# Stick-breaking weights with the query in the partitions: key sums by a scan on VectorE, and the logarithms transposed

## The chip, the core and the metric

The kernel runs on one core of one Trainium2 chip. The metric is the device time of one execution in microseconds; the median of three runs of the kernel before is 400.91 (400.55 to 401.03).

## What is computed

Two layers over 256 tokens of width 1024. In each layer a mixer of three groups of heads (block-sparse attention "moba", differential attention "diff", stick-breaking attention), gated and projected back, then a cross-attention to 256 memory tokens; at the end an RMS norm. The part that changes is stick-breaking, with 6 heads of width 64:

```
def stick_breaking_attention(q, k, v):
    """A[t,s] = sigmoid(z_ts) * prod_{s<j<t} (1 - sigmoid(z_tj)), strictly causal, no positions."""
    ...
        z = jnp.einsum('bhqd,bhkd->bhqk', qi, k).astype(jnp.float32) * scale
        mask = kpos[None, :] < (q0 + jnp.arange(Q_BLOCK))[:, None]
        log_beta = jax.nn.log_sigmoid(z)
        log_1m_beta = jnp.where(mask, log_beta - z, 0.0)
        between = lax.cumsum(log_1m_beta, axis=3, reverse=True) - log_1m_beta
        w = jnp.where(mask, jnp.exp(log_beta + between), 0.0)
        return jnp.einsum('bhqk,bhkd->bhqd', w.astype(v.dtype), v)
```

So each score z needs the sum of softplus(z) over the keys from its own to the query: the logarithm of the weight is z less that sum.

## The kernel before

Nearly all of TensorE's work is the big projections. Each weight granule (128 x 1024, float32, 512 KB) is loaded by SP into `wraw`, rounded by ScalarE into `whi` (L156), and VectorE computes the residual `wlo = wraw - whi` (L157); a product then takes three instructions (whi with the rounded activation, wlo with it, whi with the activation's residual). `wraw` has 5 buffers, `whi` and `wlo` 6 each, and granules are asked for five ahead. In `t_stationary` (L455 to L457, the token-major projections T0 to T3) a granule is 12 products of 512 columns.

TensorE's order is written out by hand: the projections call `tick` after each few products with the nanoseconds they took, and `tick` runs the steps of the attention jobs that are due. A job is a Python generator; each `yield` gives TensorE's time of the step and the wait until the next one is due (`SB_WAIT`, `PT_WAIT` and so on, in nanoseconds, L58 to L72). The other engines' orders come from the framework's scheduler, and each engine works through its own in order.

A stick-breaking job `sb(c, last)` (L745) does one pair of heads: three per layer, so six in all. Its steps are:

- `stick_banks` (L619): four score products in float32 into two banks of PSUM, with the key in the partitions and the query along the row (128 x 384: 256 queries for the first 128 keys, the later 128 for the rest), and a mask added by a product with an identity (L633).
- `softplus` (L637): per bank four Exp, Ln and Abs instructions on ScalarE (L642 to L646), three on VectorE (L647 to L649), and a split into a rounded part `sbh` (ScalarE) and a residual `sbl` (VectorE, L170).
- `stick_weights` (L655): the sum over keys goes down the partitions, so it is a product with a triangle of -1 (`trim`, L659) and, across the two key blocks, with a full matrix of -1 (`allm`, L660), for both parts, added on top of the scores in the same bank; then an Exp to SBUF gives the weights (`pt`).
- `pv` (L602): the product with the values, for all waiting pairs together.

The diff and moba attentions (`score_quad`, `score_banks`, `numerators`) have the query in the partitions; their probabilities are transposed by TensorE in `p_transposed` (L591): three 128 x 128 transposes into a bank and a copy. The tiles `sbe`, `sby` and so on come from the pool `work`, which has two buffers of each name.

Of the kernel before, what the change touches and what calls it, by code (L numbers as in the profile page):

```python
# [15 lines left out]
OP = mybir.AluOpType  # L16
# [4 lines left out]
KT = 8  # L21
NEG = -1.0e30
# [36 lines left out]
SB_WAIT, SB_PACE = 8000, 9000  # L59
# [18 lines left out]
class Trunk:  # L78
# [94 lines left out]
    def constants(self):  # L173
# [3 lines left out]
        self.identR = C.tile([128, 128], R, name="identR")  # L177
        nc.gpsimd.tensor_copy(self.identR, self.ident)
        tmp = self.work.tile([128, 256], F32, name="ctmp", tag="sq")

        self.cmask = C.tile([128, 384], F32, name="cmask")
        nc.gpsimd.memset(self.cmask, 0.0)
        for c in (0, 256):
            nc.gpsimd.affine_select(self.cmask[:, c:c + 128], self.cmask[:, c:c + 128], [[-1, 128]],
                                    OP.is_ge, NEG, base=0, channel_multiplier=1)

        nc.gpsimd.memset(tmp, 0.0)
        for c in (0, 128):
            nc.gpsimd.affine_select(tmp[:, c:c + 128], tmp[:, c:c + 128], [[1, 128]],
                                    OP.is_gt, NEG, base=0, channel_multiplier=-1)  # L190
        self.smask = C.tile([128, 256], R, name="smask")
        nc.gpsimd.tensor_copy(self.smask, tmp)

        tri = C.tile([128, 128], F32, name="trif")
        nc.gpsimd.memset(tri, -1.0)
        self.allm = C.tile([128, 128], R, name="allm")
        nc.gpsimd.tensor_copy(self.allm, tri)

        self.halfm = C.tile([128, 128], R, name="halfm")
        half = self.work.tile([128, 256], F32, name="ctmp2", tag="sq")  # L200
        nc.gpsimd.memset(half[:, 0:128], -1.0)
# [3 lines left out]
        nc.gpsimd.affine_select(tri, tri, [[-1, 128]], OP.is_ge, 0.0, base=0, channel_multiplier=1)  # L205
        self.trim = C.tile([128, 128], R, name="trim")
        nc.gpsimd.tensor_copy(self.trim, tri)
# [348 lines left out]
    def score_banks(self, qa, ka, qb, kb):  # L556

        a, b = self.bank(), self.bank()
        near = lambda ps, q, k: self.nc.tensor.matmul(ps[:, 0:128], q[:, 0:128], k[:, 0:128], start=True, stop=True)
        far = lambda ps, q, k: self.nc.tensor.matmul(ps[:, 128:384], q[:, 128:256], k, start=True, stop=True)  # L560
        near(a, qa, ka)
        far(b, qb, kb)
        far(a, qa, ka)
        near(b, qb, kb)
        return a, b

    def score_quad(self, qk):

        banks = [self.bank() for _ in qk]
        for a, b in ((0, 128), (128, 256)):  # L570
            for ps, (q, k) in zip(banks, qk):
                self.nc.tensor.matmul(ps[:, a:a + b], q[:, a:a + 128], k[:, 0:b], start=True, stop=True)
        return banks

    def numerators(self, ps, scale):
# [4 lines left out]
        for t, c in ((0, slice(0, 128)), (1, slice(128, 384))):  # L580
# [4 lines left out]
        for t, c in ((0, slice(0, 128)), (1, slice(128, 384))):  # L585
# [5 lines left out]
    def p_transposed(self, p):  # L591
# [6 lines left out]
        with self.urgent():  # L598
            nc.scalar.activation(pt[:, 0:384], ps[:, 0:384], AF.Copy)
        return pt  # L600

    def pv(self, v, pts):  # L602
# [16 lines left out]
    def stick_banks(self, qa, ka, qb, kb):  # L619

        nc = self.nc
        a, b = self.bank(), self.bank()
        kw = dict(skip_group_check=True)
        near = lambda ps, q, k, s: nc.tensor.matmul(ps[:, 0:256], k[:, 0:128], q, start=s, stop=False, **kw)
        far = lambda ps, q, k, s: nc.tensor.matmul(ps[:, 256:384], k[:, 128:256], q[:, 128:256], start=s, stop=False,
                                                   **kw)
        far(a, qa, ka, True)
        near(b, qb, kb, True)
        near(a, qa, ka, False)
        far(b, qb, kb, False)  # L630
        for ps in (a, b):
            diagonal = ps.rearrange("p (b c) -> p b c", c=256)[:, :, 0:128]
            nc.tensor.matmul(diagonal, self.identR, self.smask, start=False, stop=True, **kw)  # L633
        return a, b

    def softplus(self, ps):

        nc = self.nc
# [7 lines left out]
        nc.scalar.activation(r, y, AF.Exp, scale=-1.0)  # L646
        nc.vector.scalar_tensor_tensor(r, e, 1.0, r, OP.add, OP.mult)  # L647
        nc.vector.scalar_tensor_tensor(r, r, -1.0, y, OP.add, OP.add)
        nc.vector.scalar_tensor_tensor(e, z, 0.0, r, OP.max, OP.add)  # L649
        self.split(e, hi, lo)  # L650
        return ps, hi, lo

    def stick_weights(self, ps, hi, lo):

        nc = self.nc  # L655
        kw = dict(skip_group_check=True)
        z = ps[:, 0:384]
        for p in (hi, lo):
# [478 lines left out]
```

## Time and profile before

| what | value |
|---|---|
| median of the runs | 400.91 us |
| profiled execution, its own time | 399.81 us |
| its span, first to last instruction | 398.1 us |
| TensorE busy | 390.6 us, 2803 products |
| VectorE busy | 320.8 us, 784 instructions |
| ScalarE busy | 282.4 us, 593 instructions |
| granted TensorE clock, mean | 0.999 |

The profile is of one execution. Busy time counts an engine's instructions, with overlaps once; a product's recorded length includes its drain, so what a product costs the stream is the distance from its start to the next one's. "Idle before" a row names what ended the wait of that engine. A chain of waits leads back from the last instruction to what released it.

### The profile page before, as it was taken

What the parts mean: (1) busy time and instruction counts of PE and PEld (TensorE: products, weight loads), DVE (VectorE), ACT (ScalarE), POOL (GpSimd) and SP (SyncE); (2) the same over time, 40 slices, a digit from 0 to 9 for tenths busy, and PEclk for the clock granted to TensorE, in tenths of its full rate; (3) what the DMA queues carried; (4) which work ended last, traced back from release to release, by engine and by line L of the source; (5) the groups of instructions that cost most, each with busy time, mean ns of one, the idle gap of its engine ahead of it and who ended that gap; (6) DMA issues with size and microseconds to landing.
All of it is one profiled execution on the core that took longest, in us unless ns stands there. A gap on an engine that the chain in (4) does not pass through costs nothing.

```text
span 398.1 us, 7706 instructions
## 1 busy us (share of the span) xinstructions
PE 390.6 (98%) x2803; PEld 355.2 (89%) x2803; DVE 320.8 (81%) x784; ACT 282.4 (71%) x593; POOL 43.7 (11%) x109
## 2 busy tenths in 40 slices
PE   8999999999999999999999999999999999999993
PEld 8999988777899989988999999888788999998983
DVE  5988868788969869889797864876997896797964
ACT  7889588776866868559486934879687667675843
POOL 5688950000000000000000000000000000000000
PEclk9999999999999999999999999999999999999999
DMA  8995794334353343721747765443346433361002
GB/s 287 351 321 173 244 314 151 132 108 138 131 186 130 107 156 109 239 80 53 265 121 267 242 210 169 160 158 105 94 154 225 132 120 127 108 212 53 1 2 105
DMA packets 19190, 64.10 MB, mean 161 GB/s; under 512 B 2384, under 2 KB 2768, under 8 KB 19152
## 3 DMA queue, kind: packets, MB, share of 16 engines
q1 hardware_dynamic: 19152, 63.61, 47.2%
q8 instruction: 22, 0.36, 0.4%
q14 instruction: 16, 0.13, 0.1%
HBM read 62.55 MB, written 1.05 MB: 160 GB/s over the span
## 4 chain that ended last, share of the span: by engine, by line
PE 89%; DVE 6%; ACT 3%; issue 1%; ACTq 0%; DVEq 0%
PE bank L428 39%; PE bank L455 8%; PE bank L457 7%; PE bank L456 7%; PE bank L1013 3%; PE bank L607 2%; PE bank L596 2%; DVE wlo L157 2%; PE bank L948 1%; PE bank L659 1%; ACT whi L156 1%; PE bank L765 1%; PE bank L483 1%; PE bank L482 1%; PE bank L481 1%
## 5 line engine op out<-in xcount | busy, mean ns | idle before, releaser
L157 DVE TENSOR_TENSOR wlo<-wraw,whi 128x1024 fp32r<-128x1024 f32 (+2 forms) x118 | 137.3, 1169 | 33.8 <-ACT whi L156 32.3
L156 ACT ACTIVATE whi<-wraw 128x1024 fp32r<-128x1024 f32 (+2 forms) x118 | 118.2, 1011 | 40.0 <-PE bank L428 19.5
L428 PE MATMUL bank<-xh,whi 128*128 128x256 f32 x416 | 119.1, 287 | 0.0
L428 PE MATMUL bank<-xh,wlo 128*128 128x256 f32 x416 | 117.3, 283 | 0.0
L428 PE MATMUL bank<-xl,whi 128*128 128x256 f32 x416 | 117.1, 283 | 0.0
L428 PEld LDWEIGHTS bank<-xh,whi 128*128 128x128 f32 x416 | 79.4, 191 | 1.4 <-issue 0.7
L428 PEld LDWEIGHTS bank<-xh,wlo 128*128 128x128 f32 x416 | 79.5, 192 | 0.2 <-DVE wlo L157 0.2
L428 PEld LDWEIGHTS bank<-xl,whi 128*128 128x128 f32 x416 | 79.5, 192 | 0.0
L455 PE MATMUL bank<-whi,xh 128*128 128x512 f32 x128 | 52.0, 407 | 0.0
L456 PE MATMUL bank<-wlo,xh 128*128 128x512 f32 x128 | 50.1, 392 | 0.0
L457 PE MATMUL bank<-whi,xl 128*128 128x512 f32 x128 | 50.1, 391 | 0.0
L586 ACT ACTIVATE prob<-prob,mx 128x128 f32<-128x128 f32 (+1 forms) x56 | 24.8, 445 | 10.9 <-DVE mx L583 10.9
L455 PEld LDWEIGHTS bank<-whi,xh 128*128 128x128 f32 x128 | 24.1, 188 | 6.2 <-issue 2.0
L457 PEld LDWEIGHTS bank<-whi,xl 128*128 128x128 f32 x128 | 24.0, 188 | 5.3
L456 PEld LDWEIGHTS bank<-wlo,xh 128*128 128x128 f32 x128 | 24.1, 188 | 4.1
L314 ACT ACTIVATE xh<-h 128x256 fp32r<-128x256 f32 x32 | 14.5, 497 | 6.6 <-DVE h L310 6.3
L428 PE MATMUL bank<-mh,whi 128*128 128x256 f32 x64 | 18.8, 294 | 0.0
L581 DVE CUSTOM_DVE_ANT_0 prob<-bank,cmask 128x128 f32<-128x128 f32 (+1 forms) x56 | 17.9, 350 | 0.3
L428 PE MATMUL bank<-ml,whi 128*128 128x256 f32 x64 | 18.1, 282 | 0.0
L428 PE MATMUL bank<-mh,wlo 128*128 128x256 f32 x64 | 18.1, 282 | 0.0
L325 ACT ACTIVATE sq<-h 128x256 f32<-128x256 f32 x28 | 11.4, 410 | 6.4 <-DVE sqacc L326 5.9
L647 DVE SCALAR_TENSOR_TENSOR sbr<-sbe,sbr 128x384 f32<-128x384 f32 x12 | 6.4, 556 | 11.7 <-ACT sbr L646 11.7
(285 smaller groups left out, 790.2 us busy)
## 6 DMA issues: line engine op xcount, KB each, us to landing
wraw<-in_w_dram SPq DMA_DIRECT2D x107, 512.0 KB, 3.8
wraw<-in_w_dram SPq DMA_DIRECT2D x10, 256.0 KB, 4.4
wraw<-in_memT_dram SPq DMA_DIRECT2D x4, 512.0 KB, 4.6
h<-in_xT_dram SPq DMA_DIRECT2D x3, 256.0 KB, 4.5
out_dram<-wraw SPq DMA_DIRECT2D x2, 288.0 KB, 2.2
wraw<-in_gfin_dram SPq DMA_DIRECT2D x1, 512.0 KB, 4.9
out_dram<-wraw SPq DMA_DIRECT2D x2, 224.0 KB, 2.2
h<-in_xT_dram SPq DMA_DIRECT2D x1, 280.0 KB, 3.0
```

The costliest lines, as they stand in the source:

```text
L156: nc.scalar.activation(hi[:, c], raw[:, c], AF.Copy)
L157: nc.vector.tensor_tensor(lo[:, c], raw[:, c], hi[:, c].bitcast(F32), OP.subtract)
L314: nc.scalar.activation(h, src[k], AF.Copy, scale=g)
L325: nc.scalar.activation(s, src[k], AF.Square)
L428: nc.tensor.matmul(outs[m], st[:, kk, c], x[k], start=k + p == 0 and m % 2 == 0, stop=k == n - 1 and p == 2, skip_group_check=True)
L455: nc.tensor.matmul(outs[t], xh[k][:, c], whi[:, kk, :], start=first, stop=False)
L456: nc.tensor.matmul(outs[t], xh[k][:, c], wlo[:, kk, :], start=False, stop=False)
L457: nc.tensor.matmul(outs[t], xl[k][:, c], whi[:, kk, :], start=False, stop=last)
L581: nc.vector.tensor_tensor_reduce(s[:, c], ps[:, c], self.cmask[:, c], 1.0, -3.0e38, OP.add, OP.max, accum_out=m[:, t:t + 1])
L586: nc.scalar.activation(s[:, c], s[:, c], AF.Exp, bias=m[:, t:t + 1], scale=scale, accum_out=sm[:, t:t + 1])
L596: nc.tensor.transpose(ps[:, b * 128:b * 128 + 128], p[:, b * 128:b * 128 + 128], self.ident)
L1013: nc.tensor.matmul(out[:, 0:w], x[:, r], w_, start=m == 0 and not seeded, stop=m == 11, skip_group_check=True)
```

## The change

Stick-breaking's scores are made with the query in the partitions and the key along the row, by the same `score_banks` that moba uses. The tokens are laid out backwards on the host (input, positions, and output turned around), so that the sum from a key to the query becomes a running sum along the row; all other masks and block positions are turned to match, in `SEG`. `stick_logs` takes the place of `softplus`: VectorE adds the mask to the scores as it reads the bank (`sbz`), ScalarE does Abs, Exp, Ln, Exp and a Relu, VectorE two combining instructions, then one scan per query block (`tensor_tensor_scan` over Relu and the rest, 256 and 128 columns), and the subtract from the scores. The logarithms are then transposed by TensorE, and the instruction that takes them out of PSUM is an Exp (`p_transposed` with `AF.Exp`). Products with the mask, with `trim` and `allm`, and the split in two parts are gone. `SB_WAIT` goes from 8000 to 9000, the wait before the value products from `PT_WAIT` (950) to `SB_PT` (1300), and the job's stated TensorE times from 1070 and 1070 to 760 and 660.

```
+SEG = (0, slice(0, 256)), (1, slice(256, 384))
...
-SB_WAIT, SB_PACE = 8000, 9000
+SB_WAIT, SB_PACE, SB_PT = 9000, 9000, 1300
...
     def score_banks(self, qa, ka, qb, kb):
         a, b = self.bank(), self.bank()
-        near = lambda ps, q, k: self.nc.tensor.matmul(ps[:, 0:128], q[:, 0:128], k[:, 0:128], start=True, stop=True)
-        far = lambda ps, q, k: self.nc.tensor.matmul(ps[:, 128:384], q[:, 128:256], k, start=True, stop=True)
+        near = lambda ps, q, k: self.nc.tensor.matmul(ps[:, 256:384], q[:, 128:256], k[:, 128:256], start=True, stop=True)
+        far = lambda ps, q, k: self.nc.tensor.matmul(ps[:, 0:256], q[:, 0:128], k, start=True, stop=True)
...
-    def p_transposed(self, p):
+    def p_transposed(self, p, func=AF.Copy):
...
-            nc.scalar.activation(pt[:, 0:384], ps[:, 0:384], AF.Copy)
+            nc.scalar.activation(pt[:, 0:384], ps[:, 0:384], func)
...
-    def softplus(self, ps):
+    def stick_logs(self, ps):
         nc = self.nc
-        z = ps[:, 0:384]
-        W = lambda n, dt=F32: self.work.tile([128, 384], dt, name=n)
-        e, y, r, hi, lo = W("sbe"), W("sby"), W("sbr"), W("sbh", R), W("sbl", R)
+        W = lambda n: self.work.tile([128, 384], F32, name=n)
+        z, e, y, r, u = W("sbz"), W("sbe"), W("sby"), W("sbr"), W("sbu")
+        nc.vector.tensor_tensor(z, ps[:, 0:384], self.smask, OP.add)
         nc.scalar.activation(e, z, AF.Abs)
         nc.scalar.activation(e, e, AF.Exp, scale=-1.0)
         nc.scalar.activation(y, e, AF.Ln, bias=1.0)
         nc.scalar.activation(r, y, AF.Exp, scale=-1.0)
+        nc.scalar.activation(u, z, AF.Relu)
         nc.vector.scalar_tensor_tensor(r, e, 1.0, r, OP.add, OP.mult)
         nc.vector.scalar_tensor_tensor(r, r, -1.0, y, OP.add, OP.add)
-        nc.vector.scalar_tensor_tensor(e, z, 0.0, r, OP.max, OP.add)
-        self.split(e, hi, lo)
-        return ps, hi, lo
-
-    def stick_weights(self, ps, hi, lo):
...
+        for _, c in SEG:
+            nc.vector.tensor_tensor_scan(y[:, c], u[:, c], r[:, c], 0.0, OP.add, OP.add)
+        nc.vector.tensor_tensor(z, z, y, OP.subtract)
+        return z
...
         def sb(c, last):
             qk = [x[64 * j:64 * j + 64] for j in range(2) for x in (sqk[c], sqk[3 + c])]
-            z = [self.softplus(ps) for ps in self.stick_banks(*qk)]
-            yield 1070, SB_WAIT
-            w = [self.stick_weights(*x) for x in z]
-            yield 1070, PT_WAIT
+            z = [self.stick_logs(ps) for ps in self.score_banks(*qk)]
+            yield 760, SB_WAIT
+            w = [self.p_transposed(x, AF.Exp) for x in z]
+            yield 660, SB_PT
...
-    x = tr(f("x")[0]).reshape(128, 4, 512)
+    x = tr(f("x")[0][::-1]).reshape(128, 4, 512)
```

VectorE's order in the changed kernel, layer 0, from the second pair's first combining step to its last subtract (`sbz_1093` and `sbz_1109` are the pair's two banks; the two rows to `sby` of 256 and 128 columns are the scans of a bank; `wlo` rows belong to the projections):

```order
L619 SCALAR_TENSOR_TENSOR sbr_1096<-sbe_1094,sbr_1096 128x384
L620 SCALAR_TENSOR_TENSOR sbr_1096<-sbr_1096,sby_1095 128x384
L622 SCALAR_TENSOR_TENSOR sby_1095<-sbu_1097,sbr_1096 128x256
L622 SCALAR_TENSOR_TENSOR sby_1095<-sbu_1097,sbr_1096 128x128
L619 SCALAR_TENSOR_TENSOR sbr_1112<-sbe_1110,sbr_1112 128x384
L623 TENSOR_TENSOR sbz_1093<-sbz_1093,sby_1095 128x384
L620 SCALAR_TENSOR_TENSOR sbr_1112<-sbr_1112,sby_1111 128x384
L159 TENSOR_TENSOR wlo_1179<-wraw_1177,whi_1178 128x1024
L622 SCALAR_TENSOR_TENSOR sby_1111<-sbu_1113,sbr_1112 128x256
L622 SCALAR_TENSOR_TENSOR sby_1111<-sbu_1113,sbr_1112 128x128
L159 TENSOR_TENSOR wlo_1197<-wraw_1195,whi_1196 128x1024
L623 TENSOR_TENSOR sbz_1109<-sbz_1109,sby_1111 128x384
```

The same place before, from the second pair's first combining step to the residuals of its two banks:

```order
L647 SCALAR_TENSOR_TENSOR sbr_1116<-sbe_1114,sbr_1116 128x384
L647 SCALAR_TENSOR_TENSOR sbr_1130<-sbe_1128,sbr_1130 128x384
L648 SCALAR_TENSOR_TENSOR sbr_1116<-sbr_1116,sby_1115 128x384
L648 SCALAR_TENSOR_TENSOR sbr_1130<-sbr_1130,sby_1129 128x384
L649 SCALAR_TENSOR_TENSOR sbe_1114<-bank_1106,sbr_1116 128x384
L649 SCALAR_TENSOR_TENSOR sbe_1128<-bank_1107,sbr_1130 128x384
L157 TENSOR_TENSOR wlo_1184<-wraw_1182,whi_1183 128x1024
L170 TENSOR_TENSOR sbl_1118<-sbe_1114,sbh_1117 128x384
L170 TENSOR_TENSOR sbl_1132<-sbe_1128,sbh_1131 128x384
```

Between the combining steps and a bank's end there was one `wlo`; now there are two, and the second bank's end stands behind both.

VectorE's order in the changed kernel just ahead of that, from the first pair's last rows to the second pair's mask adds (L612, which read the score banks):

```order
L159 TENSOR_TENSOR wlo_1038<-wraw_1036,whi_1037 128x1024
L623 TENSOR_TENSOR sbz_1002<-sbz_1002,sby_1004 128x384
L159 TENSOR_TENSOR wlo_1071<-wraw_1069,whi_1070 128x1024
L536 TENSOR_TENSOR rp1_1128<-tq_1125,cosr_250 128x128
L388 COPY rbcm_1157<-bank_1154 128x256
L612 TENSOR_TENSOR sbz_1093<-bank_1087,smask_125 128x384
L612 TENSOR_TENSOR sbz_1109<-bank_1088,smask_125 128x384
```

The mask adds are new on this engine; they stand behind the first pair's last subtract, a weight residual, a product of the rotary embedding and a copy.

TensorE's order in the changed kernel, from the third pair's scores in layer 0 to the transposes of the second pair (`ident,sbz`), and what follows:

```order
L547 MATMUL bank<-sqk_687,sqk_684 128x128
L548 MATMUL bank<-sqk_687,sqk_684 128x256 x2
L547 MATMUL bank<-sqk_687,sqk_684 128x128
L443 MATMUL bank<-whi,xh_292 128x512
L444 MATMUL bank<-wlo,xh_292 128x512
L445 MATMUL bank<-whi,xl_293 128x512
L443 MATMUL bank<-whi,xh_292 128x512
L444 MATMUL bank<-wlo,xh_292 128x512
L445 MATMUL bank<-whi,xl_293 128x512
L584 MATMUL bank<-ident,sbz 128x128 x6
L725 MATMUL bank<-ident,tq 128x128 x4
```

Before, the mask product (L633) followed the scores, and in the place of the six transposes stood eight products with `trim` and `allm`. The scores of the next pair stand six big products ahead of a pair's transposes. In layer 0 the first pair's transposes stand at the like place behind the second pair's scores, where before the eight products came ahead of those scores.

## Rows read from the trace of the kernel before

**Rows 1.** The page, part 1: busy us, share of the span, instructions of each engine.

```profile
PE 390.6 (98%) x2803; PEld 355.2 (89%) x2803; DVE 320.8 (81%) x784; ACT 282.4 (71%) x593; POOL 43.7 (11%) x109
```

**Rows 2.** The page, part 4: the chain that ended last, by engine.

```profile
PE 89%; DVE 6%; ACT 3%; issue 1%; ACTq 0%; DVEq 0%
```

**Rows 3.** Windows: length, busy of PE, PEld, DVE, ACT, POOL, clock, DMA, GB/s.

```profile
74.00:90.00 16.00, 16.00 (x110) 12.44 (x109) 12.21 (x40) 12.85 (x33) 0.00 (x0) 1.00 0.41 133
...
275.00:290.00 15.00, 15.00 (x99) 11.40 (x97) 13.76 (x50) 10.13 (x26) 0.00 (x0) 1.00 0.37 121
```

**Rows 4.** Timeline of TensorE, first pair of layer 0: start us, length us, instruction.

```profile
54.22 0.39 PE L457 MATMUL bank<-whi,xl 128*128 128x512 f32 x1
...
55.39 0.51 PE L633 MATMUL bank<-smask,identR 128*128 128x256 f32 x2
55.73 0.39 PE L455 MATMUL bank<-whi,xh 128*128 128x512 f32 x1
```

**Rows 5.** Timeline of TensorE, the second pair's sum products in layer 0.

```profile
76.08 0.40 PE L457 MATMUL bank<-whi,xl 128*128 128x512 f32 x1
76.32 0.34 PE L659 MATMUL bank<-sbh,trim 128*128 128x384 f32 x1
...
77.41 0.60 PE L765 MATMUL bank<-ident,tq 128*128 128x128 f32 x4
```

**Rows 6.** Timeline of TensorE, three transposes among big products.

```profile
99.41 0.49 PE L596 MATMUL bank<-ident,prob 128*128 128x128 f32 x3
99.65 0.48 PE L455 MATMUL bank<-whi,xh 128*128 128x512 f32 x1
99.97 0.39 PE L456 MATMUL bank<-wlo,xh 128*128 128x512 f32 x1
```

**Rows 7.** Timeline of TensorE: first sum product, value products, difference scores of layer 0.

```profile
64.16 0.34 PE L659 MATMUL bank<-sbh,trim 128*128 128x384 f32 x1
...
79.33 0.65 PE L607 MATMUL bank<-pt,sv 128*64 128x256 f32 x4
...
81.12 0.40 PE L456 MATMUL bank<-wlo,xh 128*128 128x512 f32 x1
...
85.32 0.94 PE L572 MATMUL bank<-dT,dT 32*128 32x128 f32 x16
```

**Rows 8.** Groups of VectorE by shape: count, busy us, mean ns, idle before.

```profile
L157 DVE TENSOR_TENSOR wlo<-wraw,whi 128x1024 fp32r<-128x1024 f32 x107 | 130.3, 1223 | 30.7 <-ACT whi L156 29.2 <-PE bank L660 0.9
...
L170 DVE TENSOR_TENSOR sbl<-sbe,sbh 128x384 fp32r<-128x384 f32 x12 | 6.5, 553 | 0.0
...
L548 DVE TENSOR_TENSOR rp<-tq,cosr 128x128 f32<-128x128 f32 x4 | 1.2, 290 | 2.1 <-ACT tq L725 2.1
```

**Rows 9.** Timeline of ScalarE in layer 0: start us, length us, instruction, idle before.

```profile
57.40 0.94 ACT L644 ACTIVATE sby<-sbe 128x384 f32<-128x384 f32 x2
58.22 0.93 ACT L646 ACTIVATE sbr<-sby 128x384 f32<-128x384 f32 x2
...
87.25 0.40 ACT L586 ACTIVATE prob<-prob,mx 128x128 f32<-128x128 f32 x1 [1.33 <-DVE mx L583]
```

**Rows 10.** Timeline of VectorE in layer 0.

```profile
55.73 1.23 DVE L157 TENSOR_TENSOR wlo<-wraw,whi 128x1024 fp32r<-128x1024 f32 x1 [0.78 <-ACT whi L156]
...
73.56 1.02 DVE L170 TENSOR_TENSOR sbl<-sbe,sbh 128x384 fp32r<-128x384 f32 x2
...
78.36 0.56 DVE L647 SCALAR_TENSOR_TENSOR sbr<-sbe,sbr 128x384 f32<-128x384 f32 x1 [2.64 <-ACT sbr L646]
78.96 0.56 DVE L648 SCALAR_TENSOR_TENSOR sbr<-sbr,sby 128x384 f32<-128x384 f32 x1
```

**Rows 11.** Windows at the end of the span: columns as in rows 3.

```profile
392.00:396.00 4.00, 0.00 (x0) 0.00 (x0) 1.53 (x6) 1.66 (x5) 0.00 (x0) 1.00 0.28 106
396.00:397.00 1.00, 0.00 (x0) 0.00 (x0) 0.00 (x0) 0.00 (x0) 0.00 (x0) 1.00 0.58 226
397.00:398.10 1.10, 0.00 (x0) 0.00 (x0) 0.00 (x0) 0.00 (x0) 0.00 (x0) 0.56 0.00 0
```

More of the change, by code (lines that the diff above doesn't have):

```diff
@@ L176, in constants @@
         make_identity(nc, self.ident)
[L177 to L195, printed above, removed]
+        self.cmask, self.smask = [C.tile([128, 384], F32, name=n) for n in ("cmask", "smask")]
+        for m, op in ((self.smask, OP.is_gt), (self.cmask, OP.is_ge)):
+            nc.gpsimd.memset(m, 0.0)
+            for c in (0, 256):
+                nc.gpsimd.affine_select(m[:, c:c + 128], m[:, c:c + 128], [[1, 128]], op, NEG, base=0,
+                                        channel_multiplier=-1)
         self.allm = C.tile([128, 128], R, name="allm")
-        nc.gpsimd.tensor_copy(self.allm, tri)
-        self.halfm = C.tile([128, 128], R, name="halfm")
         half = self.work.tile([128, 256], F32, name="ctmp2", tag="sq")
         nc.gpsimd.memset(half[:, 0:128], -1.0)
+        nc.gpsimd.tensor_copy(self.allm, half[:, 0:128])
+        self.halfm = C.tile([128, 128], R, name="halfm")
         nc.gpsimd.memset(half[0:64, 64:128], 0.0)
@@ L569, in score_quad @@
         banks = [self.bank() for _ in qk]
-        for a, b in ((0, 128), (128, 256)):
+        for t, c in SEG[::-1]:
             for ps, (q, k) in zip(banks, qk):
-                self.nc.tensor.matmul(ps[:, a:a + b], q[:, a:a + 128], k[:, 0:b], start=True, stop=True)
+                self.nc.tensor.matmul(ps[:, c], q[:, 128 * t:128 * t + 128], k[:, 128 * t:256], start=True, stop=True)
         return banks
@@ L579, in numerators @@
         m = self.work.tile([128, 2], F32, name="mx", bufs=6)
-        for t, c in ((0, slice(0, 128)), (1, slice(128, 384))):
+        for t, c in SEG:
             nc.vector.tensor_tensor_reduce(s[:, c], ps[:, c], self.cmask[:, c], 1.0, -3.0e38, OP.add, OP.max,
@@ L584, in numerators @@
         sm = self.work.tile([128, 2], F32, name="sum", bufs=6)
-        for t, c in ((0, slice(0, 128)), (1, slice(128, 384))):
+        for t, c in SEG:
             nc.scalar.activation(s[:, c], s[:, c], AF.Exp, bias=m[:, t:t + 1], scale=scale,
@@ L646, in softplus @@
         nc.scalar.activation(r, y, AF.Exp, scale=-1.0)
+        nc.scalar.activation(u, z, AF.Relu)
         nc.vector.scalar_tensor_tensor(r, e, 1.0, r, OP.add, OP.mult)
         nc.vector.scalar_tensor_tensor(r, r, -1.0, y, OP.add, OP.add)
-        nc.vector.scalar_tensor_tensor(e, z, 0.0, r, OP.max, OP.add)
-        self.split(e, hi, lo)
-        return ps, hi, lo
-    def stick_weights(self, ps, hi, lo):
[L655 to L658, printed above, removed]
-            nc.tensor.matmul(z, self.trim, p, start=False, stop=False, **kw)
-            nc.tensor.matmul(ps[:, 128:256], self.allm, p[:, 256:384], start=False, stop=p is lo, **kw)
-        w = self.work.tile([128, 512], F32, name="pt", bufs=4)
-        with self.urgent():
-            nc.scalar.activation(w[:, 0:384], z, AF.Exp)
-        return w
+        for _, c in SEG:
+            nc.vector.tensor_tensor_scan(y[:, c], u[:, c], r[:, c], 0.0, OP.add, OP.add)
+        nc.vector.tensor_tensor(z, z, y, OP.subtract)
+        return z
     def mixer(self, l):
@@ L786, in diff @@
                 nc.vector.tensor_scalar(r2, r2, self.lam[:, l:l + 1], None, OP.mult)
-                for t, cc in ((0, slice(0, 128)), (1, slice(128, 384))):
+                for t, cc in SEG:
                     nc.vector.tensor_scalar(p2[:, cc], p2[:, cc], r2[:, t:t + 1], None, OP.mult)
@@ L845, in moba @@
                 p, r = self.numerators(b, 0.125)
-                for t, cc in ((0, slice(0, 128)), (1, slice(128, 384))):
+                for t, cc in SEG:
                     nc.vector.tensor_scalar(p[:, cc], p[:, cc], r[:, t:t + 1], None, OP.mult)
@@ L1084, in _layout @@
     d = {"memT": tr(f("mem")[0]),
-         "pos": np.ascontiguousarray(f("positions")[0].reshape(2, 128).T)}
+         "pos": np.ascontiguousarray(f("positions")[0][::-1].reshape(2, 128).T)}
     cols = []
```

24 lines of the change are left out of this document (3 added, 21 removed).

## The prediction, before the changed kernel was run

> **What bounds the kernel now.** I read the page's busy lines first [rows 1]: TensorE is busy 98% of a span of 398.1 us, VectorE 81%, ScalarE 71%. Then the chain that ended last [rows 2]: 89% of it is TensorE. So what shortens TensorE's own stream shortens the kernel, as long as TensorE never waits; and whatever makes it wait is paid in full. Then the windows of two stretches with stick-breaking or the work right behind it [rows 3]: TensorE is busy all of 16.00 and 15.00 us, VectorE 12.21 and 13.76. VectorE has little room there, and it is an engine that works in its written order: an instruction that is late holds all behind it. The profiled execution took 399.81 us, 1.10 less than the median of the runs, 400.91; sums below are differences, added to the median.
>
> **What leaves TensorE, and what comes.** Stick-breaking runs for three pairs of heads in each of two layers, six times. Per pair:
> - Mask products: two, from 55.39 to 55.73 [rows 4], 0.34 us. Without them the next 512-column product pays the short gap that follows small products, 0.09 (0.32 in place of 0.23 behind the transposes of [rows 6]). Removed: 0.25 to 0.34, I take 0.30.
> - Sum products: eight, from 76.32 to 77.41 [rows 5], 1.09, with a gap behind them 1.14.
> - Added: six transposes. Three took 99.41 to 99.97 less one product of 0.23 [rows 6], 0.33; six take 0.66.
>
> A pair saves 0.30 + 1.14 - 0.66 = 0.78 us, six pairs **4.7 us**. The score products and the value products keep their number and sizes. The masks built on GpSimd at the start are fewer and lie before any use; SP's queue keeps its order. Both are costed at nothing: VectorE's first mask add comes near 57 us. ScalarE's count per bank stays: one Relu comes, one rounding copy goes.
>
> **What VectorE gets, and when TensorE needs it.** Before, ScalarE read the banks at once and VectorE had four instructions of 384 columns per bank behind it. Now it has four again and two scans, and one of the four, the mask add, comes ahead of ScalarE, so the chain begins on VectorE's queue. The chain from a pair's mask add to the second bank's subtract, in the order written (the first VectorE excerpt), costs:
> - add 0.55 [rows 8], then six ScalarE steps until the first bank's last Exp starts, 0.415 each (two equal ones span 0.94, one lasts 0.525), that Exp 0.53 [rows 9], hand-overs 0.06: 3.63.
> - two dependent VectorE steps of 0.60 (78.36 to 78.96), then three independent 384-column ones at 0.47, then the last, 0.55 [rows 10]: 3.16. So far 6.79.
> - the two scans of each bank, twice; call a bank's S. No row shows a scan. **Bounds:** VectorE's rows go from 290 ns at 128 columns to 553 at 384 [rows 8], 1.03 ns a column on 158 fixed. As one ordinary pass a 256 and a 128 column scan issue in 0.54; as two ordinary passes each, in 1.07. The operation is two additions in series per column, the second feeding the next column, in one instruction: I take two column times and one fixed part, S = 0.94, nearest to two passes.
> - weight residuals (wlo) that stand between: 1.14 each (1.23 long, issue to issue 0.09 less) [rows 8]. The order puts two between the first bank's work and the second bank's subtract for the second pair of both layers and the first of layer 1, one for the others.
>
> The Trainium skill, page "DVE: opcode table, instruction layouts, handler registers and perf-mode slots", section "Datapath and trigger behaviour", says that the built-in tensor_tensor_scan feeds back across stages and runs at half throughput. The ordinary rows alone would give 403.7, the second rival; by the rule it is about the forecast's 407.9. No row here shows which.
>
> TensorE's slot is counted in its new order from the end of a pair's scores to its second bank's transposes. Prices: big 512-column product 0.229 (36, with two transposes of 0.11 among them, fill 55.73 to 64.16), a pair's scores 0.95 (54.45 to 55.39), four value products of two pairs 1.6 (79.33 to 81.12 less 0.23), the difference scores 1.05 (0.94 and a gap) [rows 4, 7], a transpose 0.11. The second pair of layer 0 has 6 + 24 + 6 products, 2 + 6 + 3 transposes and one set of scores: 8.24 + 1.2 + 0.95 = 10.4.
>
> The lateness d is how long after the scores the mask add starts. First pair of layer 0: scores end 55.39, but the wlo of 55.73 stands ahead until 56.87 [rows 10]: d = 1.48. For the later pairs the add stands behind the pair before's last subtract and what follows it (the VectorE excerpt with the mask adds: a wlo 1.14, a rope product 0.2, a copy 0.34). So lateness is handed on. Layer 0, second pair, with S = 0.94: the first pair's subtract is off VectorE 11.55 after its own scores, plus 1.68, less the 9.45 between the two scores, is d = 3.8. The chain ends at 3.8 + 6.79 + 2.28 + 1.88 = 14.7 against a slot of 10.4 (and 0.3 already waited): **TensorE waits 4.0 us**. In the kernel before the same pair was done at 74.6 and needed at 76.32 [rows 5, 10].
>
> By the same sum, wait with S = 0.54 and with 0.94:
> - layer 0, first pair: slot 11.3; 0 and 0.3 (0.3 of norm work is on its chain).
> - layer 0, second: 2.7 and 4.0.
> - layer 0, third: its slot is pushed back by the second's wait; 0 and 0.2. Its value products follow six products later, and on ScalarE their last Exp now stands behind an Exp of the difference scores that waits for VectorE, 1.33 in [rows 9]: 1.3 in both.
> - layer 1, first: d 1.48 (a wlo ahead here too), two wlo, slot 10.9; 0.7 and 1.5.
> - layer 1, second: slot 12.0 (30 products lie ahead of the next scores); 0.3 and 1.1.
> - layer 1, third: one wlo and 0.4 of the next stage's maxima in the chain, slot 10.1; 2.5 and 3.3.
>
> Sums: 7.5 and 11.7. From S = 0.54 to 0.94 they grow by 4.2; two passes (S = 1.07) add a third of that again, 13.1. Net of the 4.7 saved: +2.8, **+7.0**, +8.4.
>
> The weights themselves don't become late: with six buffers a residual is used five granules after it is made, each 12 products of 0.229, some 13 us later, and VectorE's work grows by four scans, 1.9 us, a pair. Next late would be the difference numerators, which follow directly on VectorE; their transposes (99.41) come 14 us after their scores (85.32) [rows 6, 7], so I add nothing.
>
> **Rivals.**
> - *The chain fits its slot.* Then only TensorE's saving shows: 400.91 - 4.7 = 396.2, faster. For it: 98% busy, two engines with idle time, and the slot is lengthened by 1.5 to 2 us against 8.4 before. It needs the second pair's mask adds within 0.3 us of its scores even with cheap scans (10.4 - 6.79 - 2.28 - 1.08 = 0.3); they stand behind a wlo and the first pair's last subtract, which alone comes later. And sbz has two buffers: the adds need the first pair's transposes done, which TensorE's order puts 6 products and two transposes behind the second scores, 1.4 + 0.2 + 0.33 and a last one's 0.27 [rows 6], 2.2 us at the least. Chance 0.09.
> - *Scans as cheap as any VectorE row* (S = 0.54): waits 7.5, 403.7. Chance 0.17, with errors of the waits either way.
> - *Waits and saving cancel*: needs waits of 4.7, less than the cheap scan gives: 400.9. Chance 0.06.
> - *Scans as two passes*: 409.3. Chance 0.16.
> - *The clock falls in a wait.* After its last product TensorE sits idle from 392 on; the granted clock is still 1.00 until 397 and 0.56 (full 2.4 GHz giving way to 1.2) in the last stretch [rows 11]. The waits are under 4.1 us, shorter than that idle time. No row shows how long it would stay low; were it as long as the longest wait, 4 us (an estimate), half of that comes on top: 409.9 or above. Chance 0.05. The Trainium skill, page "TensorE: Matmul & The Clock Gate", section "Part 1: The HAM clock gate", says that an idle TensorE is throttled to half; rows 11 agree, and by it alone the loss would come on top of every long wait.
>
> **Numbers.** Forecast (S = 0.94, chance 0.47): 400.91 + 7.0 = 407.9. About 0.2%, 0.8 us, is what a measurement of this kernel can tell from no change. The range goes from 401.5, the cheap scan with 2.3 less of waiting, to 411.0, two passes with 1.7 more; it leaves out the fitting chain and part of the clock. Faster 0.09, same 0.06, slower 0.85 from the cases above.
>
> **What would show it.** Transposes of six in 0.66 and TensorE's busy sum down by some 4.7 plus its gaps: the first step. Scan rows near 0.69 and 0.42 us: S; near 0.42 and 0.29 the cheap rival. Idle time of TensorE ahead of the transposes of sbz, released by VectorE's last subtract, longest at the second pair of layer 0 and third of layer 1: the waits. If TensorE shows no such idle time, the forecast is wrong at the chain; if the idle time is there but the sum isn't, at the saving. Granted clock under 1.00 near 80 or 285 us: the last rival.

## The result, and the profile after

| | before | changed |
|---|---|---|
| median of the runs, us | 400.70 (400.37 to 401.03, 6 runs) | 411.02 (407.85 to 412.74, 6 runs) |
| ratio of the two | | 1.025, 95% interval 1.021 to 1.029 |
| profiled execution, us | 399.81 | 411.77 |
| its span, us | 398.1 | 410.0 |
| its mean granted clock | 0.999 | 0.985 |

The change makes the kernel 10.3 us slower. The forecast was 407.9 with a range up to 411.0, so the sign and the order of size were right, and the median lies on the upper edge (411.02 against 411.0). The six runs of the changed kernel are not alike, and their granted clock tells them apart: 407.85 us at a mean clock of 0.996, 409.91 and 410.35 at 0.987, 411.69 to 412.74 at 0.983 to 0.985.

The page's busy line and its chain by engine, of the changed kernel:

```profile
PE 392.7 (96%) x2779; PEld 353.6 (86%) x2779; DVE 332.8 (81%) x808; ACT 282.4 (69%) x593; POOL 42.5 (10%) x104
...
PE 71%; DVE 15%; ACT 8%; issue 4%; DMA 1%; SPq 0%; DVEq 0%; ACTq 0%
```

Against [rows 1, 2], TensorE has 24 instructions fewer and yet 2.1 us more of busy time, and its share of the chain is 71% where it was 89%. VectorE has 12 us more work, and 15% of the chain in place of 6%. What TensorE waits for, in the view of waits (engine, line, releaser: us in total, times, longest):

```profile
PE bank L584 <- DVE sbz L623: 8.4, 4, 3.5
PE bank L1024 <- DVE warm L1001: 1.2, 1, 1.2
PE bank L595 <- ACT pt L587: 1.1, 1, 1.1
PE bank L416 <- DVE wlo L159: 0.2, 1, 0.2
```

Only the second of these (the start of the program) was there before. The first is the transposes of `sbz` that wait for VectorE's last subtract, four times; the third is the value products. Idle time in this view starts at the modelled end of the last product, which lies 0.16 us behind the moment at which the next could have started (0.39 us long, 0.23 apart, or 0.27 and 0.11 for transposes). So each wait costs 0.16 more than it shows: 8.4 + 1.1 + 5 x 0.16 = 10.3 us.

That is not all that TensorE lost. The windows around the two longest waits (length; busy of PE, PEld, DVE, ACT, POOL; clock; DMA share; GB/s):

```profile
75.00:80.00 5.00, 1.50 (x10) 0.90 (x9) 5.00 (x9) 2.09 (x3) 0.00 (x0) 1.00 0.32 105
80.00:84.00 4.00, 4.00 (x17) 3.02 (x18) 1.84 (x3) 3.45 (x9) 0.00 (x0) 0.57 0.75 249
...
285.00:289.00 4.00, 1.34 (x7) 0.69 (x5) 4.00 (x10) 2.31 (x3) 0.00 (x0) 0.91 0.00 0
289.00:295.00 6.00, 5.86 (x19) 3.96 (x20) 4.54 (x26) 4.10 (x17) 0.00 (x0) 0.50 0.39 132
```

TensorE is idle for most of 75 to 80 and of 285 to 289. About when it is released (0.3 us after the first release, 0.8 us before the second) the granted clock goes from 1.00 to 0.50 (2.4 GHz to 1.2 GHz), and the next products run at half rate: 0.43 x 4.0 = 1.7 us lost from 80 to 84, and 0.50 x 6.0 = 3.0 us lost from 289 to 295, both estimates from the window's length and clock. In the kernel before the clock was 1.00 in these stages [rows 3].

The sum for the profiled executions, 411.77 - 399.81 = 12.0: waits 10.3, half-rate products 4.7, and so 3.0 is left as TensorE's saving. These are two single executions, and the opening of the program took 0.5 us longer in the second (see the first experiment); without it the saving is 3.5.

Two more views show the chain that is waited for. VectorE's groups by shape (count, busy us, mean ns, idle before):

```profile
L622 DVE TENSOR_TENSOR_SCAN sby<-sbu,sbr 128x256 f32<-128x256 f32 x12 | 8.3, 688 | 0.2
...
L612 DVE TENSOR_TENSOR sbz<-bank,smask 128x384 f32<-128x384 f32 x12 | 6.2, 550 | 0.0
...
L622 DVE TENSOR_TENSOR_SCAN sby<-sbu,sbr 128x128 f32<-128x128 f32 x12 | 4.8, 401 | 0.0
```

VectorE's timeline for the second pair of layer 0 (start us, us, instruction, idle before):

```profile
66.78 0.55 DVE L623 TENSOR_TENSOR sbz<-sbz,sby 128x384 f32<-128x384 f32 x1
67.25 1.22 DVE L159 TENSOR_TENSOR wlo<-wraw,whi 128x1024 fp32r<-128x1024 f32 x1
...
68.92 1.01 DVE L612 TENSOR_TENSOR sbz<-bank,smask 128x384 f32<-128x384 f32 x2
...
72.55 0.56 DVE L619 SCALAR_TENSOR_TENSOR sbr<-sbe,sbr 128x384 f32<-128x384 f32 x1 [0.47 <-ACT sbr L617]
...
76.05 1.22 DVE L159 TENSOR_TENSOR wlo<-wraw,whi 128x1024 fp32r<-128x1024 f32 x1
77.18 1.00 DVE L622 TENSOR_TENSOR_SCAN sby<-sbu,sbr 128x256 f32<-128x256 f32 x2
78.10 1.20 DVE L159 TENSOR_TENSOR wlo<-wraw,whi 128x1024 fp32r<-128x1024 f32 x1
79.21 0.55 DVE L623 TENSOR_TENSOR sbz<-sbz,sby 128x384 f32<-128x384 f32 x1
```

and TensorE's timeline beside it:

```profile
64.46 0.37 PE L547 MATMUL bank<-sqk,sqk 64*128 64x128 f32 x1
...
75.81 0.52 PE L584 MATMUL bank<-ident,sbz 128*128 128x128 f32 x3
79.82 0.69 PE L584 MATMUL bank<-ident,sbz 128*128 128x128 f32 x3 [3.50 <-DVE sbz L623]
80.31 1.06 PE L725 MATMUL bank<-ident,tq 128*128 128x128 f32 x4
```

Read them together. The pair's scores start at 64.46 and take 0.95, so they are done near 65.4. The first mask add comes at 68.92, behind the pair before's last subtract (66.78), a residual and more: 3.5 us late. From then to the end of the second bank's subtract (79.76) it takes 10.8 us, with two residuals of 1.1 in between. TensorE has the first bank's transposes in place at 75.81 and then stands still until the second bank's data come. The last row shows four transposes in 1.06 us that take 0.60 elsewhere [rows 5]: half rate.

### The profile page after: what moved, and what is told of

It reads as the page before. It is cut to its first block, busy times and chain, and to the rows that moved or that the text cites. A ratio compares the mean times of both kernels' runs of the same rounds, so it can differ in the third digit from the quotient of the medians.

```text
span 410.0 us, 7670 instructions
## 1 busy us (share of the span) xinstructions
PE 392.7 (96%) x2779; PEld 353.6 (86%) x2779; DVE 332.8 (81%) x808; ACT 282.4 (69%) x593; POOL 42.5 (10%) x104
## 4 chain that ended last, share of the span: by engine, by line
PE 71%; DVE 15%; ACT 8%; issue 4%; DMA 1%; SPq 0%; DVEq 0%; ACTq 0%
PE bank L416 38%; PE bank L443 4%; PE bank L444 4%; PE bank L445 4%; DVE wlo L159 3%; DVE sby L622 3%; PE bank L973 3%; PE bank L584 2%; PE bank L595 2%; ACT whi L158 2%; DVE sbr L620 1%; PE bank L908 1%; DVE sbr L619 1%; ACT sbe L613 1%; DVE sbz L623 1%
## 5 line engine op out<-in xcount | busy, mean ns | idle before, releaser
L443 PE MATMUL bank<-whi,xh 128*128 128x512 f32 x128 | 54.2, 423 | 0.0
L444 PE MATMUL bank<-wlo,xh 128*128 128x512 f32 x128 | 51.3, 401 | 0.0
L445 PE MATMUL bank<-whi,xl 128*128 128x512 f32 x128 | 51.0, 399 | 0.0
L574 ACT ACTIVATE prob<-prob,mx 128x256 f32<-128x256 f32 (+1 forms) x56 | 24.8, 446 | 12.9 <-DVE mx L571 12.9
L587 ACT ACTIVATE pt<-bank 128x384 f32<-128x384 f32 x32 | 15.0, 480 | 12.6 <-PE bank L584 11.3
L569 DVE CUSTOM_DVE_ANT_0 prob<-bank,cmask 128x256 f32<-128x256 f32 (+1 forms) x56 | 17.9, 351 | 0.0
```

Source lines behind the costliest of these rows:

```text
L443: nc.tensor.matmul(outs[t], xh[k][:, c], whi[:, kk, :], start=first, stop=False)
L444: nc.tensor.matmul(outs[t], xh[k][:, c], wlo[:, kk, :], start=False, stop=False)
L445: nc.tensor.matmul(outs[t], xl[k][:, c], whi[:, kk, :], start=False, stop=last)
L569: nc.vector.tensor_tensor_reduce(s[:, c], ps[:, c], self.cmask[:, c], 1.0, -3.0e38, OP.add, OP.max, accum_out=m[:, t:t + 1])
L574: nc.scalar.activation(s[:, c], s[:, c], AF.Exp, bias=m[:, t:t + 1], scale=scale, accum_out=sm[:, t:t + 1])
L587: nc.scalar.activation(pt[:, 0:384], ps[:, 0:384], func)
```

## The experiments

Each edit is made to the changed kernel. Times are medians; the kernel before, run beside them on the same chip, took 400.87 (first to fourth), 400.69 (fifth to seventh) and 400.93 (eighth and ninth).

**First: TensorE's own stream alone.**

```diff
-SB_WAIT, SB_PACE, SB_PT = 9000, 9000, 1300
+SB_WAIT, SB_PACE, SB_PT = 9000, 9000, 1800
...
-        nc.scalar.activation(e, z, AF.Abs)
...
-        nc.vector.tensor_tensor(z, z, y, OP.subtract)
...
-            w = [self.p_transposed(x, AF.Exp) for x in z]
+            w = [self.p_transposed(x, AF.Relu) for x in z]
```

> Changed kernel with the logarithms, the running sums and the subtract of stick-breaking left out; the six transposes of a pair read the masked scores, their eviction takes Relu in place of Exp, and the value products come 0.5 us later in TensorE's plan. What is left is the change of TensorE's own stream. Theory (waits of TensorE on VectorE's chain plus a lower clock make up the whole loss): no wait, granted clock 1.00 throughout, and the saving stands bare. By the prediction's term of 4.7 us the time is 396.0; by the changed kernel's trace, where the differences at like places leave a saving of about 3.7, it is 397.0. Rival (TensorE's own stream got longer): 401 or more.

Measured: 397.19 (396.50 to 397.28), ratio 0.991 (0.989 to 0.992). Its busy line and its waits:

```profile
PE 387.4 (98%) x2779; PEld 350.6 (89%) x2779; DVE 304.4 (77%) x748; ACT 257.4 (65%) x533; POOL 41.0 (10%) x104
...
PE bank L1013 <- DVE warm L990: 1.2, 1, 1.2
PE bank L416 <- DVE wlo L159: 0.3, 1, 0.3
```

TensorE waits for nothing in stick-breaking, and the kernel is 3.7 us faster than before by the medians, 2.6 by the two profiled executions (397.24 against 399.81). So the change does what it is for on TensorE, and the loss is waiting and what follows it. The saving is real but under the 4.7 of the prediction. Where the rest goes shows when start-to-start times of TensorE's instructions in the two traces are added up by tile. Gone are 6.84 us of sum products and 2.05 of mask products, come are 3.61 of transposes: 5.3 saved, more than predicted. But 1.1 comes back in the 512-column products (0.75 of it in those that open a granule, as the one behind each group of transposes does), 0.7 in value products that no longer follow each other closely (one group takes 1.50 in place of 0.80), and the rest, some 0.9, in the opening of the program: some 8 us after its first product TensorE is 0.84 us behind the kernel before. In the other traces the same stretch is behind by 0.06 (fourth run) to 1.2 us (fifth), and by 1.0 in the seventh, whose opening is the same code as the fourth's. So it moves by about 1 us from execution to execution, and the one trace of the kernel before, of an execution 0.9 us under its median, has the shortest opening of all eleven traces. Without the opening the two traces give 3.5, near the 3.7 of the medians; whether any of the opening's part belongs to the change isn't settled.

**Second: keep TensorE busy in the waits.**

```diff
+        for _ in range(fill):
+            nc.tensor.matmul(ps[:, 0:256], self.warm[:, 0:128], self.warm, start=True, stop=True)
...
-            w = [self.p_transposed(x, AF.Exp) for x in z]
+            w = [self.p_transposed(x, AF.Exp, f) for x, f in zip(z, (0, {(0, 2): 20, (1, 0): 14}.get((l, c), 0)))]
```

> Changed kernel with 20 and 14 products of zeros (128x256, about 0.12 us each) put ahead of the second bank's transposes of the two pairs that wait longest (second of layer 0, third of layer 1), so that TensorE is idle for about 1.3 us there in place of 3.5 and 2.8. Nothing else changes. Theory (the clock falls because TensorE idles in these waits, and costs 1.7 and 3.0 us of half-rate products behind them): granted clock 1.00 to the end, time 411.0 - 4.7 + 0.3 = 406.6. Rival (the fall has another cause, or the slow stretch only takes up time in which TensorE would have waited later): 410.5 to 411.5.

Measured: 408.40 (408.33 to 410.43). The windows at the two places:

```profile
75.00:80.00 5.00, 4.04 (x29) 3.42 (x27) 5.00 (x9) 2.43 (x4) 0.00 (x0) 1.00 0.27 88
80.00:84.00 4.00, 3.85 (x30) 2.87 (x30) 2.57 (x5) 3.40 (x9) 0.00 (x0) 1.00 0.76 242
...
284.00:288.00 4.00, 3.23 (x22) 2.58 (x20) 4.00 (x9) 2.52 (x4) 0.00 (x0) 1.00 0.02 4
288.00:294.00 6.00, 5.74 (x30) 4.50 (x31) 5.86 (x32) 4.96 (x18) 0.00 (x0) 1.00 0.49 169
```

The clock stays at 1.00 and products of zeros, whose results nothing uses, make the kernel 2.6 us faster by the medians (span of the profiled execution 406.5 against 410.0, 3.5). The edit does nothing in these stages but fill idle time, so the trace is direct evidence that the idle time brought the clock down. The gain itself is less certain than the trace: the ratios to the kernel before, 1.020 (1.018 to 1.023) here and 1.025 (1.021 to 1.029) without the edit, overlap, one of these four runs took 410.43 at a mean clock of 0.993, and one of the changed kernel's six took 407.85 without any filling. All runs together say it more firmly: the five kernels without a wait of TensorE over 1.6 us in their traces, the start aside (first, third, fourth, seventh, ninth), had mean clocks of 0.995 to 0.999 in all 27 executions; the four with waits of 2.4 us and more (changed, fifth, sixth, eighth) had 0.982 to 0.993 in 17 of 18.

The expectation of 406.6 was too low: of the 4.7 us at half rate about 1.2 are not won. Half of that is the value products in layer 0, to which TensorE comes sooner and finds them not ready: their wait grows from 1.1 to 1.7, as the view of waits shows. Another 0.3 is the opening; the rest is not traced.

```profile
PE bank L586 <- DVE sbz L625: 4.2, 4, 1.2
PE bank L597 <- ACT pt L589: 1.7, 1, 1.7
```

With the clock kept up, the time is 408.4: the forecast of 407.9 was close to the changed kernel without the clock's fall.

**Third: no running sums.**

```diff
-        for _, c in SEG:
-            nc.vector.tensor_tensor_scan(y[:, c], u[:, c], r[:, c], 0.0, OP.add, OP.add)
-        nc.vector.tensor_tensor(z, z, y, OP.subtract)
+        nc.vector.tensor_tensor(z, z, r, OP.subtract)
...
-            w = [self.p_transposed(x, AF.Exp) for x in z]
+            w = [self.p_transposed(x, AF.Relu) for x in z]
```

> Changed kernel without the two running sums of each bank (left out; the subtract takes the result of the step before, and the eviction of the transposes takes Relu in place of Exp). Theory (the chain on VectorE is too long for its slot by the waits seen): each pair's chain is 1.9 us shorter and hands less lateness on, so the waits of 10.3 us fall to between 1.3 and 4.2, none over 2 us, and the clock stays at 1.00: 400.7 - 3.7 + 1.3 to 4.2 = 398.3 to 401.2. Rival (where the mask adds stand in VectorE's queue decides, not the scans): waits stay within 1 us of before each, 408 or more.

Measured: 401.73 (401.42 to 402.54). The waits, and VectorE at the second pair of layer 0:

```profile
PE bank L595 <- ACT pt L587: 1.9, 2, 1.2
PE bank L560 <- ACT dT L725: 1.3, 1, 1.3
PE bank L1022 <- DVE warm L999: 1.2, 1, 1.2
PE bank L584 <- ACT whi L158: 0.9, 1, 0.9
...
68.84 1.01 DVE L612 TENSOR_TENSOR sbz<-bank,smask 128x384 f32<-128x384 f32 x2
...
76.33 0.55 DVE L621 TENSOR_TENSOR sbz<-sbz,sbr 128x384 f32<-128x384 f32 x1
```

24 scans, 12 x 0.688 + 12 x 0.401 = 13.1 us of VectorE's work, take 9.3 us off the kernel. Waits of 0.9 to 1.9 us in total stay on each of three lines, one of them in a new place, the difference scores (L560), which wait for ScalarE; the time is 0.5 above the expected range for that. The rival, by which the scans' price doesn't decide, is out. But the expectation was wrong in how the scans act: the second pair's adds come no sooner (68.84 against 68.92), so the lateness handed on there is the same. The pair's chain is 2.8 us shorter (68.84 to 76.88, so 8.0 in place of 10.8): the scans' 1.9 are gone, and in the new order one residual stands between the first bank's subtract and the second's, where there were two.

**Fourth: the mask back on TensorE.**

```diff
+            self.nc.tensor.matmul(diagonal, self.identR, m, start=False, stop=True, **{k: v for k, v in kw.items() if k != "stop"})
...
-        nc.vector.tensor_tensor(z, ps[:, 0:384], self.smask, OP.add)
-        nc.scalar.activation(e, z, AF.Abs)
+        nc.scalar.activation(e, ps[:, 0:384], AF.Abs)
...
-            yield 760, SB_WAIT
+            yield 1070, SB_WAIT
```

> Changed kernel with one part undone: the mask is added by TensorE again (two more products of an identity with the mask per pair, 0.31 us), ScalarE and the last subtract read the bank, and VectorE has no mask add. Theory (the chain starts late because it begins on VectorE's queue, 3.5 us after the scores at the second pair of layer 0): TensorE gets 1.9 us longer, the waits fall from 10.3 to between 0.9 and 2.8 and the clock stays at 1.00: 400.7 - 3.7 + 1.9 + 0.9 to 2.8 = 399.8 to 401.7. Rival (VectorE's load, scans above all, is what binds; the add is only 1.1 us of it per pair): waits fall by some 1.1 us each and about 6 us stay, with one fall of the clock: 405 to 408.

Measured: 402.28 (401.64 to 402.96). The waits, and the first and last step of the chain at the second pair of layer 0:

```profile
PE bank L593 <- DVE sbz L631: 1.5, 2, 0.9
PE bank L604 <- ACT pt L596: 1.4, 2, 0.7
...
65.89 0.48 ACT L621 ACTIVATE sbe<-bank 128x384 f32<-128x384 f32 x1
...
76.23 0.55 DVE L631 TENSOR_TENSOR sbz<-bank,sby 128x384 f32<-128x384 f32 x1
```

Taking 12 adds of 0.55, or 6.6 us of VectorE's work, off its queue gains 8.7 us, although TensorE gets its 2 us of mask products back. The scans gained 9.3 for 13.1 us of work; in both sums the two falls of the clock are gone as well. So what an instruction of VectorE costs here is not its length: the add is the one on which the chain starts, and it starts late. The rows show it: the chain takes 10.9 us as in the changed kernel, but it starts 3.0 us earlier (65.89 against 68.92) and so ends 3.0 us earlier. The time is 0.6 above the expected range; the waits are at its upper end, 2.9 idle and 3.5 with what the view leaves out.

**Fifth: three buffers for sbz.**

```diff
-        W = lambda n: self.work.tile([128, 384], F32, name=n)
+        W = lambda n: self.work.tile([128, 384], F32, name=n, bufs=3 if n == "sbz" else 2)
```

> Changed kernel with three buffers in place of two for sbz, so that a pair's first mask add needs no transposes of the pair before. Rival (the two buffers hold the mask adds back, and so make the waits): the wait at the second pair of layer 0 falls from 3.5 to under 2, that at the third of layer 1 from 2.8 to under 1.5, at most one fall of the clock: 406 or less. Theory (the adds are held back by what stands ahead of them in VectorE's own order, and by its load): each of the waits stays within 0.7 us of what it was, the clock falls as before: 409 to 411.5.

Measured: 410.08 (408.22 to 411.19); the line of waits, 0.9 under the changed kernel's, and an add:

```profile
PE bank L584 <- DVE sbz L623: 7.5, 4, 3.0
...
69.10 0.56 DVE L612 TENSOR_TENSOR sbz<-bank,smask 128x384 f32<-128x384 f32 x1
```

The first add of layer 0's second pair (the second row) starts 3.0 us after its scores in place of 3.5. The two buffers are not what holds the adds back, or only for the smaller part.

**Sixth: transposes later in TensorE's order.**

```diff
-SB_WAIT, SB_PACE, SB_PT = 9000, 9000, 1300
+SB_WAIT, SB_PACE, SB_PT = 10500, 9000, 1800
```

> Changed kernel with the transposes planned 1.5 us later behind their scores (10.5 us in place of 9) and the value products 0.5 us later behind the transposes; nothing else. If only the distance between scores and transposes of a pair counted, the waits of 1.23 and 0.87 would be gone, 3.5 and 2.8 would fall to 2.0 and 1.3, the value products would not wait: 400.9 - 3.7 + 3.6 of waits + one fall of the clock at the most = 401 to 403. Theory with lateness handed on (TensorE's later transposes of one pair also hold the sbz buffers longer, and its next pair's chain starts on VectorE no earlier): the first pair's waits go, but the second pair of both layers waits 3 us or more, and the clock falls behind it: 400.9 - 3.7 + 7 to 8 of waits + 2 to 4 of clock = 406 to 409.

Measured: 410.93 (408.78 to 411.41). Its waits and VectorE's adds for the second pair of layer 0:

```profile
PE bank L584 <- DVE sbz L623: 7.1, 2, 3.6
...
70.97 1.02 DVE L612 TENSOR_TENSOR sbz<-bank,smask 128x384 f32<-128x384 f32 x2
```

Two of four waits are gone, the two at the second pairs have become 3.6 and 3.5 us, and the clock falls behind both: the adds start 2.1 us later than at 68.92 in the changed kernel, their scores only 0.3. The median is 1.9 above the top of what was expected; the profiled execution, at a mean clock of 0.990, took 408.78, the other three ran at 0.982.

**Seventh: both edits, the fourth and the sixth.**

```diff
-SB_WAIT, SB_PACE, SB_PT = 9000, 9000, 1300
+SB_WAIT, SB_PACE, SB_PT = 10500, 9000, 1800
...
+            self.nc.tensor.matmul(diagonal, self.identR, m, start=False, stop=True, **{k: v for k, v in kw.items() if k != "stop"})
...
-        nc.vector.tensor_tensor(z, ps[:, 0:384], self.smask, OP.add)
```

> Both edits together: the mask on TensorE (as in the fourth run) and the later plan (10.5 and 1.8 us). Theory: the chain starts right behind the scores and has 1.5 us more, more than any wait that was left in the fourth run (0.9), so TensorE never waits: the fourth run's 402.3 less its waits of 2.9 (with their refill 3.3) = 399.0 to 399.4, faster than the kernel before by 0.4%. Rival (the later plan hands lateness on here too): one or two waits of 1 us stay, 400.5 to 401.5.

Measured: 399.41 (399.30 to 399.60), ratio to the kernel before 0.9966 (0.9954 to 0.9978). Its busy line, its waits, and the window in which its clock falls (clock 0.61):

```profile
PE 389.4 (98%) x2791; PEld 352.3 (89%) x2791; DVE 325.1 (82%) x796; ACT 279.3 (70%) x593; POOL 41.6 (10%) x106
...
PE bank L1032 <- DVE warm L1009: 1.2, 1, 1.2
PE bank L420 <- DVE wlo L159: 0.3, 1, 0.3
...
394.00:395.00 1.00, 0.00 (x0) 0.00 (x0) 0.00 (x0) 0.05 (x1) 0.00 (x0) 0.61 0.40 147
```

TensorE waits for nothing in stick-breaking, the granted clock is 1.00 until 2.8 us after the last product (which ends at 391.4), and the kernel is faster than the one before by 1.3 us (0.3%), with the same scans and transposes as the changed kernel.

**Eighth and ninth: what hands the lateness on.** Three sbz buffers, and the transposes planned 10.5 us behind the scores; in the ninth run 11500 stands in place of 10500.

```diff
-        W = lambda n: self.work.tile([128, 384], F32, name=n)
+        W = lambda n: self.work.tile([128, 384], F32, name=n, bufs=3 if n == "sbz" else 2)
...
-SB_WAIT, SB_PACE, SB_PT = 9000, 9000, 1300
+SB_WAIT, SB_PACE, SB_PT = 10500, 9000, 1800
```

> The longer distance of the sixth run (10.5 and 1.8 us) with three sbz buffers of the fifth. In the sixth run the second pairs' mask adds came 2 us later than in the changed kernel and the waits of 3.6 and 3.5 us stayed. If the sbz buffers handed that lateness on (the adds had to wait for the first pair's later transposes), the waits of the second pairs fall by some 2 us each, to 1.6 and less, no fall of the clock: 400.9 - 3.7 + 4 = 401 to 403. Rival (the residuals and the subtract that stand ahead of the adds in VectorE's order hand it on, whatever the buffers): 3 us or more stay at each second pair, with falls of the clock: 407 to 411.

Measured: 409.29 (407.83 to 411.40). VectorE at the second pair of layer 0:

```profile
68.81 0.55 DVE L612 TENSOR_TENSOR sbz<-bank,smask 128x384 f32<-128x384 f32 x1
...
70.41 1.22 DVE L159 TENSOR_TENSOR wlo<-wraw,whi 128x1024 fp32r<-128x1024 f32 x1
71.55 0.55 DVE L612 TENSOR_TENSOR sbz<-bank,smask 128x384 f32<-128x384 f32 x1
...
81.11 0.55 DVE L623 TENSOR_TENSOR sbz<-sbz,sby 128x384 f32<-128x384 f32 x1
```

With the third buffer the first add starts before the first pair's transposes (68.84), but VectorE's order then puts a residual ahead of the second add, and the second bank is as late as in the sixth run. The two long waits are 3.3 and 3.8. VectorE has no idle time from the first pair's last steps to this add, so it is the work ahead in its order that holds the add back; no run changes that order alone.

> As the eighth run, with the transposes planned 11.5 us behind the scores. If the wait is the chain's end less the slot's, and the lateness of the adds is set by VectorE's order alone, one us more of slot takes about 1 us or more from each wait of the second pairs (3.6 and 3.5 become 2 to 2.6), and the clock falls less often: 403 to 407. Rival (each us of slot is handed on again to the next pair's adds): the waits stay at 3 us or more, 407 to 411.

Measured: 403.26 (402.87 to 403.58). TensorE at the same place, and the end of VectorE's chain:

```profile
79.66 0.49 PE L584 MATMUL bank<-ident,sbz 128*128 128x128 f32 x3
81.75 0.52 PE L584 MATMUL bank<-ident,sbz 128*128 128x128 f32 x3 [1.60 <-ACT sbr L617]
...
81.06 0.55 DVE L623 TENSOR_TENSOR sbz<-sbz,sby 128x384 f32<-128x384 f32 x1
```

The chain ends at 81.61 as in the eighth run (81.66), TensorE's first bank comes at 79.66 in place of 77.89, and the wait falls from 3.3 to 1.6 (the view puts it down to ScalarE's L617; the row that ends as the wait ends is the subtract). At layer 1's second pair it falls from 3.8 to 1.4. The clock stays at 1.00. One us more of plan gains 6 us: the two waits get 4.2 shorter, and two falls of the clock go with them.

## Why the prediction was right, and where it was off

Its mechanism holds: TensorE's saving is outweighed by waits for a chain that begins and ends on VectorE's ordered queue.

- **The saving of 4.7** was too large: 3.7 by medians (first run), 2.6 by profiled executions, or 3.5 without the opening. The three prices were good, 6.84 and 2.05 removed against 6.84 and 1.8, and 3.61 added against 3.96. What the step left out is that the products around the new transposes (1.1 us) and the value products (0.7) are spaced wider afterwards.
- **The scan, S = 0.94.** The choice between bounds was right: 688 ns at 256 columns and 401 at 128 are 2.24 ns a column, against 1.03 for ordinary rows [rows 8]; a bank's two issue in 0.93. By the rule of the Trainium skill, page "DVE: opcode table, instruction layouts, handler registers and perf-mode slots", section "Datapath and trigger behaviour", the scan runs at half throughput; the trace agrees, at 2.2 times the time per column.
- **The waits.** By place, predicted and then measured (idle plus 0.16): layer 0 second pair 4.0 and 3.7, its value products 1.3 and 1.3; layer 1 first 1.5 and 1.4, second 1.1 and 1.0, third 3.3 and 3.0; layer 0 first and third 0.5 together, and no wait. The sum is 11.7 against 10.3. For the second pair of layer 0 the steps hold one by one: d = 3.8 against 3.5, the chain 10.95 against 10.8, the slot 10.4 against 10.7 (65.4 to 76.1).
- **The clock** is the step that failed. The prediction took from [rows 11] that the waits were "under 4.1 us, shorter than that idle time" and gave a fall a chance of 0.05 and a price of 2 us. The granted clock fell at both long waits of the profiled execution and cost 4.7 at half rate, net some 3.5 by the spans and 2.6 by the medians of the second run. The end of a program, where TensorE's last idle time was all that there was to read, is one example, not a bound: after its last product the clock stayed up for 5 us in that trace, but for 2.8 in the seventh run's. The Trainium skill, page "TensorE: Matmul & The Clock Gate", section "Part 1: The HAM clock gate (the "warmup" mystery)", says that an idle TensorE is throttled to half; the trace agrees (0.57 and 0.50 behind the long waits), and the prediction would have done better to give that rival more weight.

Too large a saving and too long waits nearly cancel, which is luck: -4.7 + 11.7 = 7.0 was forecast, -3.0 + 10.3 = 7.3 is in the trace. The difference between 407.9 and 411.0 is mostly the clock, as the run at 0.996 (407.85) and the second run (408.40) show from two sides.

Of the rivals, the chain that fits its slot needed the adds within 0.3 us of the scores; they came 3.5 late. Its argument from sbz's two buffers carried less: a third one takes 0.9 off the waits (fifth run), and what hands the lateness on is the work ahead in VectorE's order (eighth). That the lateness grows with the scans' price, a part of the prediction's sum for d, did not show: without scans the adds come at the same time (third run).

## What to carry to other kernels

Work that leaves a full engine pays only if the chain that replaces it fits the distance between its producer and its consumer in the full engine's own order; so when an operation goes to another engine, move the consumer as well, and check that the chain's first step doesn't join a long queue. Here neither edit alone was enough (402.3 and 410.9), both together beat the old kernel (399.4). And price a stall of TensorE at more than its length where the clock can fall behind it: two waits of 3.5 and 2.8 us cost another 4.7 us of half-rate work, of which filling the waits won back 2.6 to 3.5.

## What the runs showed of the hardware

- The granted clock fell in the middle of a program that keeps TensorE 96% busy. In the changed kernel this followed the waits of 3.5 and 2.8 us and not those of 1.2, 0.9 and 1.1; in the fifth run it followed waits of 3.0 and 2.4, in the second not one of 1.7. At the end of the kernel before it was still 1.00 some 5 us after the last product [rows 11], at the end of the seventh run's for 2.8 us.
- From one execution to the next the same kernel lost different amounts to it: mean clocks of 0.983 to 0.996 and 407.85 to 412.74 us, where the kernel without long waits (seventh run) stayed within 0.3 us (0.995 to 0.998).
- Products of zeros on TensorE in its idle time kept the granted clock at 1.00 in the trace, and the median was 2.6 us lower (second run).
- tensor_tensor_scan costs 2.24 ns a column on a fixed part of 0.11 us (688 - 256 x 2.24 = 115 ns, an estimate from the two rows).
